# Strassen's blocks in every matrix multiply of a conv-and-MLP layer, and all engines in source order

## The chip, the core and the metric

One core of a Trainium2 chip runs the kernel. Five engines work side by side, each through its own list of instructions in order: TensorE (PE, matrix products into PSUM banks), VectorE (DVE), ScalarE (ACT), GpSimd (POOL, idle here) and SyncE (SP, which issues the transfers). The metric is the device time of one execution in microseconds (us).

## The reference

One layer on x of 512 tokens by 2048 channels, float32 throughout:

```
h = rms_norm(x, norm_mix)
b, c, v = split(h @ w_in, 3)             # w_in: 2048 x 6144
x = x + (b * conv3(c * v)) @ w_out       # causal, 3 taps per channel; w_out: 2048 x 2048
h = rms_norm(x, norm_mlp)
x = x + (relu(h @ w1) ** 2) @ w2         # w1: 2048 x 8192, w2: 8192 x 2048
```

## The kernel before, in words

Each number of an operand is split into a high part `hi` (the rounded value, a cast on ACT) and a rest `lo` (DVE subtracts); a product is three matmuls: hi by hi, hi by lo, lo by hi. All operands are kept with channels on the partitions and tokens along the row.

The four multiplies are cut into 96 blocks of 2048 weight rows by 256 weight columns: 24 of `w_in`, 8 of `w_out`, 32 of `w1`, 32 of `w2` (4 chunks `ch` of 8). A *plain* block (`plain`, `unit`) takes 96 matmuls of 512 columns. A *fast* block (`fast`, `quarters`) is one level of Strassen's algorithm in Winograd's form. The weights' quarters and their sums S1 to S4 (on DVE) give seven operands. They meet seven *forms* of the activations: the quarters Y11, Y21, Y22 and the differences T1 to T4. Each of the seven products has 24 matmuls of 256 columns, 168 a block; their results are added in PSUM or in tile `c` on ACT (copies) and DVE (adds). Before, the 24 blocks of `w_in` and the 8 of `w_out` are plain, the 64 of `w1` and `w2` fast.

`load` fetches the weights of a block (2 MB in four DMAs, tile `r`, two of them). `operand` makes `whi` and `wlo` for one seventh (or, in a plain block, one quarter) in a ring of three tiles (`RING`): the cast of one operand has to wait until the matmuls of the third operand before it are done. The normed input stays in SBUF (`h_hi`, `h_lo`), as does the gated conv (`g_hi`, `g_lo`). `w_out`'s results leave as forms: Y11, Y21, Y22 are split at once, T1 to T4 go through DRAM (`t_mid`). `w1`'s results go to DRAM (`hidden`, eight arrays a piece); at each chunk of `w2` the seven forms are read back (`read`: one DMA of 1 MB, a cast and a subtraction of 128x2048). `differences` makes the T forms in four DVE instructions. RMS factors (`token_factors`) are applied to results, since a factor per token can be pulled out of the product. Nothing in the code fixes the order: a scheduler places each engine's instructions by their dependencies and the order of the source.

Of the kernel before, what the change touches and what calls it, by code (L numbers as in the profile page):

```python
# [36 lines left out]
def trunk_kernel(  # L37
# [33 lines left out]

    dram = ctx.enter_context(tc.tile_pool(name="dram", bufs=1, space=bass.MemoryType.DRAM))
# [10 lines left out]
    cst.tile([P, 224], F32, name="lead")  # L83
    edge = ctx.enter_context(tc.tile_pool(name="edge", bufs=1, side="right"))
    edge.tile([P, 8], F32, name="edge")
# [4 lines left out]
    ssq = cst.tile([P, S], F32, name="ssq")  # L90

# [14 lines left out]
    def squares(xk, first, pool):  # L106
        if first:
            act.activation(ssq, xk, AF.Square)
        else:
            sq = pool.tile([P, S], F32, tag="sq", name="sq")  # L110
            act.activation(sq, xk, AF.Square)
            dve.tensor_tensor(out=ssq, in0=ssq, in1=sq, op=ALU.add)

    def token_factors(pool, tag):


        total = bank()
        pe.matmul(total, ones, ssq, start=True, stop=True)
        m, t = (pool.tile([P, S], F32, tag=tag, name=n) for n in ("m", "t"))
# [23 lines left out]
    def unit(acc, r, k0, a_hi, a_lo, k_first=False):  # L143

        hi, lo = operand(r[:, k0 : k0 + QK, :], [P, QK, GC])
        js, ks = range(2), range(QK)
        for j, k in [(j, k) for k in ks for j in js] if k_first else [(j, k) for j in js for k in ks]:
            cs = slice(j * P, (j + 1) * P)
            a, b = a_hi[:, k0 + k, :], a_lo[:, k0 + k, :]
            first, last = k0 + k == 0, k0 + k == KT - 1  # L150
            pe.matmul(acc[j], hi[:, k, cs], a, start=first, stop=False)  # L151
            pe.matmul(acc[j], hi[:, k, cs], b, start=False, stop=False)  # L152
            pe.matmul(acc[j], lo[:, k, cs], a, start=False, stop=last)  # L153

    def plain(w, c0, a_hi, a_lo):
        acc = [bank() for _ in range(2)]
        r = load(w, 0, c0)
        for k0 in range(0, KT, QK):
            unit(acc, r, k0, a_hi, a_lo)
        return acc  # L160

    def quarters(r, early):
# [11 lines left out]
        tt(s_a, x21, x22, ALU.add)  # L174
        yield X11, operand(x11, shape)
        if early:
            yield X12, operand(x12, shape)
        tt(s_b, s_a, x11)
        yield S1, operand(s_a, shape)
        yield S2, operand(s_b, shape)  # L180
        tt(s_a, x12, s_b)
        yield S4, operand(s_a, shape)
        tt(x21, x11, x21)
        yield S3, operand(x21, shape)
        if not early:
            yield X12, operand(x12, shape)
        yield X22, operand(x22, shape)

    def fast(r, forms, c, early=False):


        bx, by, bz = (bank()[:, :HS] for _ in range(3))
        sums = {X11: bx, S1: bz, S2: bx, S4: bz, S3: bx, X12: by, X22: bx}
        t0, t1 = slice(0, HS), slice(HS, S)
        for i, (hi, lo) in quarters(r, early):
            acc = sums[i]
            f_hi, f_lo = forms[i]
# [5 lines left out]
            if i == X11:  # L203
                act.copy(c[:, 0, t0], acc)
            elif i == S1:
                act.copy(c[:, 1, t1], acc)
            elif i == S2:
                act.copy(c[:, 0, t1], acc)
            elif i == X22:
                act.copy(c[:, 1, t0], acc)  # L210
            else:
                o = {S4: c[:, 0, t1], S3: c[:, 1, t1], X12: c[:, 0, t0]}[i]
                dve.tensor_tensor(out=o, in0=acc, in1=o, op=ALU.add)  # L213

    def differences(q):
# [12 lines left out]
    rows = cw.tile([5 * KT, P], F32, name="rows", bufs=1)


    dve.memset(ones, 1.0)
    dve.memset(rows, 0.0)
    make_identity(nc, ident)
    act.dma_start(rows[:KT], norm_mix[0].rearrange("(k p) -> k p", p=P))
    act.dma_start(rows[KT : 2 * KT], norm_mlp[0].rearrange("(k p) -> k p", p=P))
    act.dma_start(rows[2 * KT :], conv_w[0].rearrange("t (k p) -> (t k) p", p=P))

    warm = bank()
    for _ in range(WARM):
        pe.matmul(warm[:, :P], ones, ones, start=True, stop=True)  # L240
    pc = bank()
    pe.transpose(pc[:, : 5 * KT], rows, ident[: 5 * KT, : 5 * KT])
    dve.tensor_copy(par[:, : 5 * KT], pc[:, : 5 * KT])

    parts = [D, 2 * D, 0]
    acc_n = [[bank() for _ in range(2)] for _ in range(2)]
    r_n = [wp.tile([P, KT, GC], F32, tag="r", name="r") for _ in range(2)]
    XK = XC // P
    with tc.tile_pool(name="xin", bufs=2, side="right", reuse_waits="tile") as xin:
        for c in range(D // XC):  # L250
# [10 lines left out]
            for j in range(0, XK, 2):  # L261
                xs = xin.tile([P, 2, S], F32, tag="xs", name="xs")
                for i in range(2):
                    kt = c * XK + j + i
                    pt = bank()
                    for b in range(S // P):
# [3 lines left out]
                    act.activation(h_hi[:, kt, :], pt, AF.Copy, scale=gain(0, kt))  # L270
                    dve.scalar_tensor_tensor(  # L271
                        out=h_lo[:, kt, :], in0=pt, scalar=gain(0, kt),
                        in1=h_hi[:, kt, :].bitcast(F32), op0=ALU.mult, op1=ALU.subtract,
                    )
                    dve.tensor_copy(xs[:, i, :], pt)
                    squares(xs[:, i, :], kt == 0, cw)
                nc.sync.dma_start(x_res[(c * XK + j) // 2], xs.rearrange("p i t -> p (i t)"))
            for i in range(2):
                unit(acc_n[i], r_n[i], c * XK, h_hi, h_lo, k_first=c == 0)
        token_factors(cw, "sq")  # L280

    with tc.tile_pool(name="gp", bufs=1, side="right", reuse_waits="tile") as gp:
        g_hi = gp.tile([P, KT, S], F32R, name="g_hi")
        g_lo = gp.tile([P, KT, S], F32R, name="g_lo")
        gp.tile([P, 112], F32, name="behind")


        pad = 16
        for n in range(NG):
            def part(i):  # L290
                if n == 0 and i < 2:
                    return acc_n[i]
                return plain(w_in, parts[i] + n * GC, h_hi, h_lo)

            acc_c = part(0)
            us = []
            for j in range(2):
                u = cw.tile([P, pad + S], F32, tag="u", name="u")
                dve.memset(u[:, pad - 2 : pad], 0.0)
                dve.tensor_tensor(out=u[:, pad:], in0=acc_c[j], in1=rbc, op=ALU.mult)  # L300
                us.append(u)
            acc_v = part(1)
            cvs = []
            for j in range(2):
                kt, u = n * 2 + j, us[j]
                cv = cw.tile([P, S], F32, tag="cv", name="cv")
                dve.tensor_tensor(out=cv, in0=acc_v[j], in1=rbc, op=ALU.mult)
                dve.tensor_tensor(out=u[:, pad:], in0=u[:, pad:], in1=cv, op=ALU.mult)
                act.activation(cv, u[:, pad - 2 : pad - 2 + S], AF.Copy, scale=tap(0, kt))
                for i in (1, 2):  # L310
                    dve.scalar_tensor_tensor(
                        out=cv, in0=u[:, pad - 2 + i : pad - 2 + i + S], scalar=tap(i, kt), in1=cv,
                        op0=ALU.mult, op1=ALU.add,
                    )
                dve.tensor_tensor(out=cv, in0=cv, in1=rbc, op=ALU.mult)
                cvs.append(cv)
            acc_b = part(2)
# [130 lines left out]
```

## Time and profile before

| | us |
|---|---|
| median of 3 runs (2020.28 to 2022.25) | 2021.81 |
| the profiled execution | 2022.01 |
| its span, first to last instruction | 2020.2 |
| PE busy | 1971.8 (98%) |
| DVE busy | 1416.3 (70%) |
| ACT busy | 841.9 (42%) |

The mean granted TensorE clock is 0.988 of full speed. PE works on `w_in` until about 535 us (its first two blocks are done at 62 us, beside the transposes of x), on `w_out` until 713, on `w1` until about 1350 and on the four chunks of `w2` to the end. Matmuls are pipelined: one is shown as busy from its start to its modelled end and the next starts before that, so the pace is read from a count of matmuls over a stretch and not from the duration of one.

### The profile page before, as it was taken

The numbers are of one execution on the slowest core, as the hardware profiler recorded it, in microseconds if no ns is written. First come the engines' busy times: TensorE is split into PE (matmuls) and PEld (weight loads), VectorE is DVE, ScalarE is ACT, GpSimd is POOL, SyncE is SP. The second block draws the span as 40 slices with busy tenths as digits, with TensorE's granted clock in tenths as the row PEclk, the third lists the DMA queues.
The fourth block names the chain that finished last, engine by engine and source line by source line (L and its number), as shares of the span: only waits on it lengthen the run. The fifth ranks groups of instructions, "written<-read, shape, count | busy, mean of one in ns | idle before, by whom it ended". The sixth has DMA issues, their size and how long they took to land.

```text
span 2020.2 us, 32807 instructions
## 1 busy us (share of the span) xinstructions
PE 1971.8 (98%) x14001; PEld 1843.0 (91%) x14001; DVE 1416.3 (70%) x1541; ACT 841.9 (42%) x1036; POOL 0.7 (0%) x6
## 2 busy tenths in 40 slices
PE   9999999999999979999999999989998998998998
PEld 8888888888888879999999999979998998998998
DVE  6643244334444588888888888888788879789875
ACT  5322222222233344544545445445455446446444
POOL 0000000000000000000000000000000000000000
PEclk9999999999999989999999999989999999999999
DMA  8322322322444454444454444467558448446542
GB/s 281 136 84 84 125 85 84 122 87 84 140 153 167 175 179 173 161 168 157 160 185 147 167 179 156 168 224 255 168 171 270 164 168 285 159 161 210 177 138 82
DMA packets 260113, 325.12 MB, mean 161 GB/s; under 512 B 9008, under 2 KB 242560, under 8 KB 255872
## 3 DMA queue, kind: packets, MB, share of 16 engines
q1 hardware_dynamic: 255616, 318.80, 46.0%
q10 hardware_dynamic: 4352, 4.24, 0.7%
q8 instruction: 109, 1.79, 0.4%
q14 instruction: 36, 0.29, 0.0%
HBM read 260.09 MB, written 62.91 MB: 160 GB/s over the span
## 4 chain that ended last, share of the span: by engine, by line
PE 89%; DMA 4%; DVE 3%; ACT 2%; issue 1%; SPq 0%; ACTq 0%; DVEq 0%
PE acc L200 18%; PE acc L202 18%; PE acc L201 18%; PE acc L152 11%; PE acc L153 11%; PE acc L151 11%; DMA f<-hidden 1%; DVE flo L101 1%; DMA r<-in_mlp_w_dram 1%; DVE wlo L101 1%; ACT whi L100 1%; DMA r<-in_conv_w_in_dram 1%; ACT fhi L100 1%; DMA f<-t_mid 0%; DVE c L410 0%
## 5 line engine op out<-in xcount | busy, mean ns | idle before, releaser
L200 PE MATMUL acc<-fhi,whi 128*128 128x256 f32 x3584 | 1000.3, 279 | 18.5 <-ACT fhi L100 16.4
L202 PE MATMUL acc<-fhi,wlo 128*128 128x256 f32 x3584 | 999.5, 279 | 17.0 <-DVE wlo L101 16.8
L201 PE MATMUL acc<-flo,whi 128*128 128x256 f32 x3584 | 999.0, 279 | 5.5 <-DVE flo L101 5.5
L101 DVE TENSOR_TENSOR wlo<-r,whi 128x1024 fp32r<-128x1024 f32 x384 | 468.7, 1223 | 385.7 <-ACT whi L100 376.7
L100 ACT CAST whi<-r 128x1024 fp32r<-128x1024 f32 x384 | 405.1, 1055 | 723.6 <-PE acc L152 376.3
L200 PEld LDWEIGHTS acc<-fhi,whi 128*128 128x128 f32 x3584 | 680.6, 190 | 20.2 <-ACT fhi L100 17.0
L202 PEld LDWEIGHTS acc<-fhi,wlo 128*128 128x128 f32 x3584 | 680.3, 190 | 18.7 <-DVE wlo L101 18.6
L201 PEld LDWEIGHTS acc<-flo,whi 128*128 128x128 f32 x3584 | 680.5, 190 | 8.1 <-DVE flo L101 8.0
L100 ACT CAST whi<-s 128x1024 fp32r<-128x1024 f32 x192 | 202.3, 1054 | 308.7 <-PE acc L201 219.0
L152 PE MATMUL acc<-h_lo,whi 128*128 128x512 f32 x768 | 298.8, 390 | 0.3 <-DVE h_lo L271 0.2
L153 PE MATMUL acc<-h_hi,wlo 128*128 128x512 f32 x768 | 298.8, 389 | 0.0
L151 PE MATMUL acc<-h_hi,whi 128*128 128x512 f32 x768 | 298.1, 390 | 0.5 <-ACT h_hi L270 0.4
L101 DVE TENSOR_TENSOR wlo<-s,whi 128x1024 fp32r<-128x1024 f32 x192 | 234.9, 1223 | 50.9 <-ACT whi L100 50.9
L152 PEld LDWEIGHTS acc<-h_lo,whi 128*128 128x128 f32 x768 | 144.1, 188 | 31.7 <-DVE h_lo L271 1.5
L151 PEld LDWEIGHTS acc<-h_hi,whi 128*128 128x128 f32 x768 | 143.8, 188 | 31.1 <-ACT h_hi L270 0.8
L153 PEld LDWEIGHTS acc<-h_hi,wlo 128*128 128x128 f32 x768 | 144.1, 188 | 29.8
L213 DVE TENSOR_TENSOR c<-acc,c 128x256 f32<-128x256 f32 x192 | 81.1, 423 | 76.9 <-PE acc L202 76.2
L151 PE MATMUL acc<-g_hi,whi 128*128 128x512 f32 x256 | 99.6, 389 | 0.0
L152 PE MATMUL acc<-g_lo,whi 128*128 128x512 f32 x256 | 99.6, 389 | 0.0
L153 PE MATMUL acc<-g_hi,wlo 128*128 128x512 f32 x256 | 99.6, 389 | 0.0
L172 DVE TENSOR_TENSOR s<-r 128x1024 f32<-128x1024 f32 x64 | 78.1, 1220 | 7.1 <-DMA r<-in_mlp_w_dram 6.4
L172 DVE TENSOR_TENSOR s<-r,s 128x1024 f32<-128x1024 f32 x64 | 78.4, 1225 | 2.0
(66 smaller groups left out, 1002.2 us busy)
## 6 DMA issues: line engine op xcount, KB each, us to landing
r<-in_mlp_w_dram SPq DMA_DIRECT2D x256, 512.0 KB, 5.5
r<-in_conv_w_in_dram SPq DMA_DIRECT2D x96, 512.0 KB, 6.0
hidden<-q SPq DMA_DIRECT2D x32, 1024.0 KB, 3.9
f<-hidden SPq DMA_DIRECT2D x28, 1024.0 KB, 6.9
r<-in_conv_w_out_dram SPq DMA_DIRECT2D x32, 512.0 KB, 5.6
xt<-x_mid SPq DMA_DIRECT2D x32, 512.0 KB, 4.3
x_mid<-c SPq DMA_DIRECT2D x24, 512.0 KB, 2.9
xn<-in_x_dram SPq DMA_DIRECT2D x16, 256.0 KB, 5.0
```

Source lines behind the costliest of these rows:

```text
L100: act.copy(hi, src)
L101: dve.tensor_tensor(out=lo, in0=src, in1=hi.bitcast(F32), op=ALU.subtract)
L151: pe.matmul(acc[j], hi[:, k, cs], a, start=first, stop=False)
L152: pe.matmul(acc[j], hi[:, k, cs], b, start=False, stop=False)
L153: pe.matmul(acc[j], lo[:, k, cs], a, start=False, stop=last)
L172: dve.tensor_tensor(out=o, in0=a, in1=b, op=op)
L200: pe.matmul(acc, hi[:, k, :], f_hi[:, k, :], start=first, stop=False, skip_group_check=True)
L201: pe.matmul(acc, hi[:, k, :], f_lo[:, k, :], start=False, stop=False, skip_group_check=True)
L202: pe.matmul(acc, lo[:, k, :], f_hi[:, k, :], start=False, stop=last, skip_group_check=True)
L213: dve.tensor_tensor(out=o, in0=acc, in1=o, op=ALU.add)
```

## The change

88 of the 96 blocks are now fast. Plain are the two blocks of `w_in` in the prologue, two more at the start of `w_in` and its last, the first and the last of `w_out` and the first of `w1`.

The forms live in fixed places: `quart` holds the four quarters, `sums` T2 and T3, `last_sum` T4; T1 shares the place of Y12. A plain block reads all four quarters, a fast one Y11, Y21, Y22 and T1 to T4. For the fast blocks of `w_in`, `x` is read back from `x_res`, scaled and subtracted into T1 to T4 (`fetch_h`, `normed_quarter`, `settle_h`). The gated conv goes out to DRAM (`gated`) and the input of the MLP too (`normed`), with their differences; `pass_over` reads each back while the plain blocks on either side of the border run. `exchange` does it for `w2`.

The work is a list of `steps`, a seventh of a fast block or a quarter of a plain one. All engines' instructions are given in source order (`tc.manual_schedule()`): in iteration i come the matmuls of step i, the outputs of step i-1, the weights' sum of step i+3, the operand of step i+2, and whatever `at(i, ...)` put there (loads, reads, splits, what follows a block).

```diff
+LEAD = 2
+HOME = {Y11: 0, Y12: 1, T1: 1, Y21: 2, Y22: 3}
-    t_mid = dram.tile([NP, P, 4, HS], F32, name="t_mid")
+    gated = dram.tile([NP, P, 8, HS], F32, name="gated")
+    normed = dram.tile([NP, P, 8, HS], F32, name="normed")
+    quart = [cst.tile([P, 4, NP, HS], F32R, name=f"q_{n}") for n in ("hi", "lo")]
+    sums = [cst.tile([P, 2, NP, HS], F32R, name=f"t_{n}") for n in ("hi", "lo")]
+    last_sum = [cst.tile([P, NP, HS], F32R, name=f"u_{n}") for n in ("hi", "lo")]
...
     def differences(q):
-        for o, a, b in ((4, 1, 0), (5, 3, 4), (6, 3, 1), (7, 2, 5)):
-            dve.tensor_tensor(out=q[:, o, :], in0=q[:, a, :], in1=q[:, b, :], op=ALU.subtract)
+        tt(slice(4, 8, 2), slice(1, 4, 2), slice(0, 2))
+        tt(5, 3, 4)
+        tt(7, 2, 5)
...
+        at(loads[-2]["end"] - LEAD - 1 if len(loads) > 1 else -1, lambda: box.update(r=load(w, r0, c0)))
...
+        for i in (X11, X12, S2, S1, S3, S4, X22) if late else range(7):
+            steps.append((
+                lambda i=i: add(i),
+                lambda i=i: box["made"][1][i](),
+                lambda op, i=i: multiply(op, i),
+                lambda i=i: out(i),
+            ))
...
+    def pass_over(last, first, src):
+        s, f, box = last["start"], first["start"], {}
+        at(s - 2, fetch_pairs, box, src, 0, 2)
+        at(s, fetch_pairs, box, src, 2, 2)
+        at(s + 1, settle_pairs, box, 0, 2)
+        at(s + 1, fetch_pairs, box, src, 4, 2)
+        at(s + 2, settle_pairs, box, 2, 2)
+        at(s + 3, settle_pairs, box, 4, 2)
+        at(s + 3, fetch_pairs, box, src, 6, 1)
+        at(f, settle_pairs, box, 6, 1)
+        at(f, settle_last, last)
+        box = {}
+        at(f + 1, fetch, box, src, T2)
+        at(f + 2, fetch, box, src, T3)
+        at(f + 3, settle, box, T2)
+        at(f + 3, fetch, box, src, T1)
+        at(f + 3, settle, box, T3)
+        at(f + 3, fetch, box, src, T4)
+        at(f + 4, settle, box, T1)
+        at(f + 6, settle, box, T4)
+    def exchange(start, src, reads):
+        for i in range(7):
+            at(start + reads[i], fetch, box, src, i)
+        for i, t in enumerate((2, 3, 4, 6, 9, 10, 11)):
+            at(start + t, settle, box, i)
+    def conv(n, box_c, box_v, d):
...
+        at(e, product)
+        at(e + d, factor)
+        at(e + d + 1, taps)
+    def gate(n, box_v, box, d):
...
+            tt(box["c"], box["c"], box_v["cv"], ALU.mult)
+            tt(q[:, :4, :].rearrange("p (i h) t -> p i (h t)", h=2), box["c"], wide(rbc), ALU.mult)
+        at(box["end"] + d, product)
+        at(box["end"] + d, lambda: differences(box["q"]))
+        at(box["end"] + d + 1, keep, box, gated[n])
...
+    with tc.manual_schedule():
+        extra(-1)
+        made = []
+        for i in range(-LEAD - 1, len(steps)):
+            if i >= 0:
+                steps[i][2](made.pop(0))
+            if i >= 1:
+                steps[i - 1][3]()
+            if i + LEAD + 1 < len(steps):
+                steps[i + LEAD + 1][0]()
+            if 0 <= i + LEAD < len(steps):
+                made.append(steps[i + LEAD][1]())
+            if i >= 0:
+                extra(i)
```

What stands on the engines in a row changes at three places. The first is DVE at the border between two chunks of `w2`, before: `flo<-f` is the split of a form, `wlo` the split of an operand, L172 a sum of weights, L213 an add of a result, L410 the residual.

```order
L172 TENSOR_TENSOR r<-r 128x8x128
L101 TENSOR_TENSOR flo<-f,fhi 128x2048
L101 TENSOR_TENSOR wlo<-r,whi 128x1024
L101 TENSOR_TENSOR flo<-f,fhi 128x2048
L213 TENSOR_TENSOR c<-acc,c 128x256
L101 TENSOR_TENSOR wlo<-r,whi 128x1024 x2
L213 TENSOR_TENSOR c<-acc,c 128x256
L101 TENSOR_TENSOR flo<-f,fhi 128x2048
L213 TENSOR_TENSOR c<-acc,c 128x256
L101 TENSOR_TENSOR flo<-f,fhi 128x2048 x2
L410 TENSOR_TENSOR c<-c,xt 128x1024
```

The same place in the changed kernel, where L179 is the sum, L279 the add, L357 the residual and `q_lo`, `t_lo` the forms:

```order
L357 TENSOR_TENSOR c<-c,xt 128x1024
L121 TENSOR_TENSOR q_lo<-f,q_hi 128x2048
L121 TENSOR_TENSOR wlo<-r,whi 128x1024
L121 TENSOR_TENSOR q_lo<-f,q_hi 128x2048
L279 TENSOR_TENSOR c<-acc,c 128x256
L121 TENSOR_TENSOR wlo<-r,whi 128x1024
L121 TENSOR_TENSOR t_lo<-f,t_hi 128x2048
L279 TENSOR_TENSOR c<-acc,c 128x256
L179 TENSOR_TENSOR s<-r 128x1024
L121 TENSOR_TENSOR wlo<-r,whi 128x1024
L279 TENSOR_TENSOR c<-acc,c 128x256
L179 TENSOR_TENSOR s<-s,r 128x1024
```

Before, the seven forms stand within 15 rows, two of them side by side; now within 25, with the split of an operand between any two.

The second is DVE in the stage of `w_in`, before, in plain blocks (L300 scales a result by the factor of its token, `u` and `cv` are the conv):

```order
L101 TENSOR_TENSOR wlo<-r,whi 128x1024 x3
L300 TENSOR_TENSOR u<-acc,rbc 128x512 x2
L101 TENSOR_TENSOR wlo<-r,whi 128x1024 x4
L307 TENSOR_TENSOR cv<-acc,rbc 128x512
L308 TENSOR_TENSOR u<-u,cv 128x512
```

And now, around the end of a trio of fast blocks (L357 the gate's two products, L193 the differences):

```order
L121 TENSOR_TENSOR wlo<-r,whi 128x1024
L357 TENSOR_TENSOR c<-c,cv 128x1024
L357 TENSOR_TENSOR q<-c,rbc 128x1024
L193 TENSOR_TENSOR q<-q 128x2x256
L193 TENSOR_TENSOR q<-q 128x256 x2
L121 TENSOR_TENSOR wlo<-r,whi 128x1024
L279 TENSOR_TENSOR c<-acc,c 128x256
L121 TENSOR_TENSOR wlo<-r,whi 128x1024
L279 TENSOR_TENSOR c<-acc,c 128x256
L179 TENSOR_TENSOR s<-r 128x1024
```

The sums of weights and the adds of results have come into this stage; there were none.

The third is SP at the border from `w_out` to `w1`, before (`xt` the residual's tiles):

```order
L134 DMA r<-in_mlp_w_dram 128x4x256 x4
L349 DMA x_mid_67<-xt 128x1024
L354 DMA t_mid<-q 128x1024
L365 DMA f<-t_mid 128x8x256 x4
L134 DMA r<-in_mlp_w_dram 128x4x256 x4
L407 DMA xt<-x_mid_67 128x1024 x2
```

And in the changed kernel at the border from `w_in` to `w_out`, which now works in the same way:

```order
L311 DMA f<-gated 128x1024
L360 DMA gated<-q 128x2048
L302 DMA f<-gated 128x8x256
L403 DMA xt<-x_res 128x2x512
L146 DMA r<-in_conv_w_out_dram 128x4x256 x4
L302 DMA f<-gated 128x8x256 x3
```

The four reads of differences stood in one piece behind the last write; now the first stands ahead of the next weights and three behind them.

## Rows read from the trace of the kernel before

**Rows 1.** Page, part 1: busy time (share of span) and instructions.

```profile
PE 1971.8 (98%) x14001; PEld 1843.0 (91%) x14001; DVE 1416.3 (70%) x1541; ACT 841.9 (42%) x1036; POOL 0.7 (0%) x6
```

**Rows 2.** Busy time of each engine in stretches; instructions in brackets, then clock, DMA.

```profile
core 0: us, PE busy (x) PEld busy (x) DVE busy (x) ACT busy (x) POOL busy (x), PEclk, DMA share, GB/s
75.00:320.00 245.00, 245.00 (x1083) 202.86 (x1082) 97.72 (x119) 57.68 (x61) 0.00 (x0) 1.00 0.30 101
...
713.00:750.00 37.00, 26.46 (x173) 23.65 (x172) 32.22 (x33) 19.67 (x22) 0.00 (x0) 0.82 0.53 176
750.00:1330.00 580.00, 580.00 (x5076) 580.00 (x5075) 502.36 (x576) 283.32 (x362) 0.00 (x0) 1.00 0.47 167
1330.00:1400.00 70.00, 56.33 (x444) 55.04 (x444) 58.40 (x56) 37.66 (x39) 0.00 (x0) 0.90 0.77 257
...
1500.00:1560.00 60.00, 54.28 (x451) 53.28 (x450) 56.62 (x48) 35.58 (x38) 0.00 (x0) 0.97 0.76 257
...
1660.00:1720.00 60.00, 54.06 (x442) 53.41 (x442) 56.31 (x47) 35.25 (x38) 0.00 (x0) 0.94 0.81 271
...
1820.00:1880.00 60.00, 54.78 (x452) 54.33 (x451) 55.89 (x49) 35.38 (x37) 0.00 (x0) 0.94 0.65 220
```

**Rows 3.** Who PE waited for: total us, times, longest.

```profile
PE acc L202 <- DVE wlo L101: 16.8, 5, 5.4
PE acc L200 <- ACT fhi L100: 16.4, 3, 8.3
PE acc L201 <- DVE flo L101: 5.5, 4, 2.3
```

**Rows 4.** PE in order of time, first transposes, third block's start: start us, duration.

```profile
8.81 1.91 PE L267 MATMUL acc<-ident,xn 128*128 128x128 f32 x16
...
62.25 0.80 PE L151 MATMUL acc<-h_hi,whi 128*128 128x512 f32 x1
```

**Rows 5.** Chain that ended last, in order of time: a finish, the tail.

```profile
1892.14 0.87 PE acc L394 x8
...
2012.73 0.38 ACT c L210
```

**Rows 6.** DVE in order of time, 1000 to 1020 us: start, duration, idle before.

```profile
1003.00 1.22 DVE L379 SCALAR_TENSOR_TENSOR c<-c,rbc 128x1024 f32<-128x1024 f32 x1
1004.14 1.22 DVE L172 TENSOR_TENSOR s<-r 128x1024 f32<-128x1024 f32 x1
...
1006.41 1.09 DVE L219 TENSOR_TENSOR q<-q 128x256 f32<-128x256 f32 x3
1007.41 1.22 DVE L172 TENSOR_TENSOR s<-s,r 128x1024 f32<-128x1024 f32 x1
```

**Rows 7.** DVE in order of time, 1365 to 1380 us.

```profile
1376.44 2.29 DVE L101 TENSOR_TENSOR flo<-f,fhi 128x2048 fp32r<-128x2048 f32 x1
1378.64 0.42 DVE L213 TENSOR_TENSOR c<-acc,c 128x256 f32<-128x256 f32 x1
```

**Rows 8.** ACT in order of time, 1505 to 1512 us.

```profile
1507.46 1.94 ACT L100 CAST fhi<-f 128x2048 fp32r<-128x2048 f32 x1
1509.27 0.40 ACT L208 COPY c<-acc 128x256 f32<-128x256 f32 x1
1509.53 1.09 ACT L100 CAST whi<-r 128x1024 fp32r<-128x1024 f32 x1
```

**Rows 9.** Chain at the border to w1: write and read of t_mid.

```profile
719.48 2.67 DMA t_mid<-q
...
722.71 7.89 DMA f<-t_mid
```

**Rows 10.** Stretches of 10 us at a border of w2, columns as in rows 2.

```profile
1520.00:1530.00 10.00, 5.00 (x27) 4.58 (x27) 9.88 (x8) 5.94 (x6) 0.00 (x0) 0.83 1.07 376
1680.00:1690.00 10.00, 4.62 (x32) 4.41 (x32) 9.21 (x8) 5.92 (x6) 0.00 (x0) 0.80 1.09 369
```

More of the change, by code (lines that the diff above doesn't have):

```diff
@@ L187, in quarters @@
[L187 to L193, printed above, removed]
-        t0, t1 = slice(0, HS), slice(HS, S)
-        for i, (hi, lo) in quarters(r, early):
-            acc = sums[i]
-            f_hi, f_lo = forms[i]
+        add = {
+            S1: lambda: tt(s_a, x21, x22, ALU.add),
+            S2: lambda: tt(s_b, s_a, x11),
+            S4: lambda: tt(s_a, x12, s_b),
+            S3: lambda: tt(x21, x11, x21),
+        }
@@ new lines, in fast, with add, multiply @@
+    def fast(w, r0, c0, late=False):
+        box = new_block(w, r0, c0, 7)
+        t0, t1 = slice(0, HS), slice(HS, S)
+        def add(i):
+            if "made" not in box:
+                box["made"] = quarters(box["r"])
+            if late and i in (S1, S2):
+                if i == S2:
+                    box["made"][0][S1]()
+                    box["made"][0][S2]()
+            else:
+                box["made"][0].get(i, lambda: None)()
+        def multiply(op, i):
+            if i == X11:
+                bx, by, bz = (bank()[:, :HS] for _ in range(3))
+                box["acc"] = {X11: bx, S1: bz, S2: bx, S4: bz, S3: bx, X12: by, X22: bx}
+            acc = box["acc"][i]
+            hi, lo = op
+            f_hi, f_lo = form(i)
@@ L228, in trunk_kernel @@
[L228 to L241, printed above, removed]
@@ L359, in trunk_kernel @@
-    fb = ctx.enter_context(tc.tile_pool(name="fb", bufs=1, side="right", reuse_waits="tile"))
-    home = {i: fa if i in (Y11, Y21, Y22) else fb for i in range(7)}
-    def read(i, src, pool):
-        f = pool.tile([P, NP, HS], F32, tag="q", name="f", bufs=3)
-        nc.sync.dma_start(f, src.rearrange("k p t -> p k t"))
-        made = form(home[i], i)
-        split(*made, f)
-        return made
-    mw = ctx.enter_context(tc.tile_pool(name="mw", bufs=2, reuse_waits="tile"))
-    for i, k in ((T1, 0), (T2, 1), (T3, 2), (T4, 3)):
-        forms[i] = read(i, t_mid[:, :, k, :], mw)
@@ new lines, in normed_quarter @@
+    def normed_quarter(box, i):
+        for k in range(NP):
+            act.activation(box[i][:, k, :], box[i][:, k, :], AF.Copy, scale=gain(0, 2 * k + (i in (Y21, Y22))))
+    boxes = [{"end": 0}, {"end": 0}]
+    at(0, early)
+    trios = []
+    for n in range(NG):
+        trio = []
+        for i in range(3):
+            if n == 0 and i < 2:
+                trio.append(boxes[i])
+            elif (n, i) in ((0, 2), (1, 0), (NG - 1, 2)):
+                trio.append(plain(w_in, 0, parts[i] + n * GC))
+            else:
+                trio.append(fast(w_in, 0, parts[i] + n * GC, late=(n, i) == (1, 1)))
+            if i == 1:
+                conv(n, *trio, 0 if n in (0, NG - 1) else 2)
+        gate(n, *trio[1:], 0 if n in (0, NG - 1) else 2)
@@ new lines, in trunk_kernel @@
+    for n in range(NG):
+        if n in (0, NG - 1):
+            box = plain(w_out, 0, n * GC)
+        else:
+            box = fast(w_out, 0, n * GC, late=n == 1)
+        if n == 0:
+            pass_over(in_last, box, gated)
+        if n == NG - 1:
+            back = {}
+            at(box["start"] - 8, fetch, back, gated, Y12)
+            at(box["start"] - 4, settle, back, Y12)
+        residual(n, box, 0 if n >= NG - 2 else 2)
+    for n in range(DFF // GC):
+        last, box = box, fast(w1, 0, n * GC, late=n == 1) if n else plain(w1, 0, n * GC)
+        if n == 0:
+            pass_over(last, box, normed)
+            at(box["start"] + 2, token_factors, lambda name: tile_x(name)[:, 0, :S])
+        if n == DFF // GC - 1:
+            exchange(box["start"], hidden[0], (-2, -1, 2, 3, 4, 5, 6))
+        squared_relu(n, box)
```

430 lines of the change are left out of this document (251 added, 179 removed).

## The prediction

> **What bounds the kernel now.** First the page: PE is busy for 98% of the span, DVE for 70%, ACT for 42% [rows 1]. So TensorE is the bound, and two questions follow: how many matmuls at which pace, and where PE stands still.
>
> The pace comes from the stretches [rows 2]. From 75 to 320 us there are only plain blocks and PE never pauses: 245 us / 1083 = 0.2262 us a matmul, 96 x 0.2262 = 21.72 us a plain block. From 750 to 1330 us there are only fast blocks: 580 us / 5076 = 0.1143 us, 168 x 0.1143 = 19.20 us a fast block, 19.20 / 7 = 2.74 us a step. That pace already holds whatever small waits a block has.
>
> The standstills come from the same view. In the five stretches at the borders the time is longer than matmuls x 0.1143: 37 - 173 x 0.1143 = 17.2 us (`w_out` to `w1`), 70 - 444 x 0.1143 = 19.3 (`w1` to `w2`), and 8.5, 9.5 and 8.3 between the chunks of `w2`: 62.8 us in all. The waits of PE name the culprits [rows 3]: operands and forms that ACT and DVE had not made, 38.7 us; the rest is the lower clock after a pause (0.80 to 0.83 in such a stretch [rows 10]).
>
> The account closes. The third block's first matmul starts at 62.25 us [rows 4]. After it come 30 plain blocks (651.6), 64 fast (1228.8), the transposes of eight finished column blocks (8 x 0.87 = 7.0 [rows 5]), the 62.8 of standstill, and the tail of 2020.2 - 2012.7 = 7.5 us [rows 5]: 2020.0 of 2020.2 us.
>
> **The change part by part.**
>
> *24 blocks made fast.* 24 x (21.72 - 19.20) = -60.4 us. Nothing covers this term: PE is the bound in those stretches [rows 2]. It supposes that the form's place and the stage don't matter to a matmul; the shapes are those of the fast blocks now.
>
> The weight loads beside the matmuls are busy for all of the 580 us in the fast stretch, against 202.86 of 245 in the plain one [rows 2]: a matmul of 256 columns has as many weights to load as one of 512. The Trainium skill (TensorE: Matmul & The Clock Gate, section on the back-to-back issue gap) gives N/2.4 + 2.5 ns a matmul, so 215.8 and 109.2 ns, where the rows have 226 and 114; by the page a swap would bring 24 x (20.72 - 18.35) = 56.9 us in place of 60.4. The measured paces decide.
>
> *The same work moved onto DVE.* A fast block costs DVE 11 full-width instructions (7 splits, 4 sums) and 3 adds. DVE starts such instructions 1.14 us apart although each is shown with 1.22; three of a quarter's width take 1.00, so 0.33 each, and a split of a form 2.20 [rows 6, 7]. A fast block is 11 x 1.14 + 3 x 0.33 = 13.5 us of DVE; a trio of `w_in` adds the product, the factor, four taps of half width (at most 1.14 each), the gate's two products and the differences (1.3): 40.6 + 2.3 + 4.6 + 2.3 + 1.3 = 51.1 us at most, against 57.6 us of PE. In `w1` a block has 13.5 + 1.14 + 1.3 = 16 of 19.2, and there PE doesn't wait [rows 2]. So I cost this at nothing. The worst step is the gate's: 1.14 + 2.28 + 1.3 = 4.7 us against 2.74; the 2.0 too much are gone two steps later, where DVE has 1.14 a step. An operand is made two steps ahead, so it may be late by 2 x 2.74 less its own chain of at most 2.7: 2.8 us. If this cover fails, the loss is that of the rival below. Even with the full 1.22 in place of 1.14 a trio stays under 57.6.
>
> *Start of the fast blocks in `w_in`.* Reading x back and making T1 to T4 stands on ACT and DVE beside eight plain steps of 21.72 / 4 = 5.43 us. What falls into the first fast steps is two form splits and one difference of that width, 6.6 us, beside 1.14 to 2.6 a step: the lag reaches about 4.4 us at the third fast step, with 2.8 to 4 free. I take 1 us (0 to 6.6). The head up to 62.25 us keeps its instructions and their order.
>
> *`exchange`, three times in `w2`.* From the step of the first form's split to the end of the next block are 12 steps, 32.9 us of PE. DVE has there the splits of 12 operands, 8 sums, 2 residuals, 7 forms and 6 adds: step by step 4.5, 3.3, 3.7, 2.6, 4.8, 2.3, 2.3, 4.5, 3.3, 3.7, 2.6, 2.6 = 40.2 us. That is 7.3 too much. Of it 2.3 us is hidden by the lead: the product X22 may not write its bank before DVE has added S3 from it, one step (2.74) less the add's 0.42. So 5 us are lost, plus about 1 for forms that are themselves late (T3, Y21 and T4 are split only two steps before their use): 6 us each, 18 in all, against 26.3 now. Bounds: 0 (the spreading hides all) and 9.5 each, as now. The transfers hardly decide: two blocks' weights (2.1 MB each), seven forms (1.05 each) and four residual tiles (0.5 each) are 13.6 MB in the 15 steps or 41 us from the first read on, 330 GB/s, where the transfers reached 376 [rows 10]; that is near enough that a late read could add 1 or 2 us.
>
> *`w1` to `w2`.* The same, but the last two blocks of `w1` also bring two times 1.3 us of differences into the 12 steps: 6 + 2.6 = 8.6, against 19.3 now, of which some 8 was a single wait for a form's cast (16.4 us in three such waits [rows 3]); `exchange` reads the first form four steps ahead of its split. Bounds 5 and 19.3.
>
> *`pass_over`, `w_in` to `w_out`.* New. The quarters come back during plain steps, where DVE has 1.14 + 2.2 of 5.43 us. The differences are the critical part: the last gate ends about 7 us into the first plain block, its write and the read of T2 take 10.9 us as at `t_mid` [rows 9], so T2 is there at 18, and T3 behind it and behind 2 MB of weights (3 MB at up to 376 GB/s [rows 10]) at 24 to 26. ACT stands at T3's cast (1.81 [rows 8]) with the operand of the second next step queued behind it, so that operand is ready at about 29 and is due at 4 x 5.43 + 2 x 2.74 = 27.2. With T4's split and the first residual in the step after (7 us of DVE), I take 4 us. Bounds: 0, and 17.2 as at the `t_mid` border, which has the same write and read without plain steps to cover them.
>
> *`pass_over`, `w_out` to `w1`.* The same with the RMS factors' chain in it, some 6.5 us of DVE two steps before T2's split, and two sums of weights: 7 us, for 17.2 now. Bounds 0 and 17.2.
>
> *Transfers and SP.* All stand in source order. A block's weights are asked for as soon as their tile is free, eight steps (22 us) before their first use, for 2.1 MB, which is 16 us even at the 7.9 us that a read of 1 MB took [rows 9]; a wait ahead of them in SP's row would have to pass 6 us to matter.
>
> **The sum.** 62.25 + 6 x 21.72 (130.3) + 88 x 19.20 (1689.6) + 7.0 + 7.5 = 1896.7 us, and standstills of 1 + 4 + 7 + 8.6 + 18 = 38.6: a span of 1935.3 us. The profiled execution lies 1.8 us over its span (2022.01 against 2020.2), and 0.2 over the median: 1937 us.
>
> **The rivals.**
>
> *The borders stay as dear as now* (and the new one costs 17.2): 1896.7 + 62.8 + 17.2 + 1.8 = 1978 us. For it: DVE has the same forms to split, and DVE was the last to arrive in most waits [rows 3]. Against: plain blocks now lie at two borders, and the forms are spread.
>
> *The borders are hidden nearly whole*: standstills of 8 us, 1907 us. For it: ACT and DVE are free for a good part of the block before. Against: 40.2 us of DVE in 32.9 us of PE.
>
> *The clock falls at the new borders.* A pause of some 5 us was followed by 0.80 to 0.83 of full clock over 10 us, i.e. 3.4 to 4 us at the lower of the two levels (1.2 GHz) and 1.7 to 2 us lost [rows 10]. If each of the 20 or so short pauses of the new kernel did this, it would be 40 us: 1977 us. Against: those 1 to 2 us pauses are not the 5 us ones of the rows. The Trainium skill (TensorE: Matmul & The Clock Gate, section on a second failure mode) describes such frequent short pauses between groups of matmuls as enough to make the clock swing; no row here shows it.
>
> *Source order lets DVE set the pace in every fast block: slower.* In iteration i the sum and the operand stand behind an output that waits for PE, so DVE cannot work ahead of the ring. As soon as DVE's work and waits in a block pass 19.2 us, each of the 88 blocks is paced by DVE; the gain of 85 us is gone when a block takes 19.20 + 85 / 88 = 20.2 us, or 0.14 us a step. With a block at 20.5 us: 2049 us. Against: 16 us in the heaviest block, and `w1` runs without a wait today at that load [rows 2].
>
> **How the numbers follow.** Forecast 60%; borders as now 14%, hidden 12%, clock 5%, slower 5%, and 4% for a failure of the swap itself (fast blocks in `w_in` no quicker than plain ones), about 2000 us. A measurement tells 0.2% (4 us) from no change. All but the slower rival and a share of the last are faster: 0.93 faster, 0.02 same, 0.05 slower. Range: from 1905, the hidden borders, to 1982, which takes in the dear ones and the clock.
>
> **What would show it.** Right: 88 blocks at 19.2 us in every stretch without a border, `w_in`'s too; PE's waits only at the six borders, by name for the splits of operands and forms, 30 to 50 us in all; the clock at 1.00 between. Wrong: a stretch of `w_in` with fast blocks over 19.5 us and PE waiting for DVE; a first wait of 5 us or more at a border on a read or a write of DRAM; a clock under 0.95 in a stretch of `w_in`.

## The result, and the profile after

The changed kernel takes 2008.94 us (median of 3 runs, 2008.15 to 2011.45) against 2021.81: a ratio of 0.9941 with an interval of 0.9918 to 0.9964, 0.6% faster. The forecast was 1937 us, its range 1905 to 1982: the sign was right, the time is 72 us above it and outside the range. The profiled execution took 2011.45 us, its span is 2009.6.

First the page's busy times, which answer to [rows 1]:

```profile
PE 1938.7 (96%) x15729; PEld 1890.8 (94%) x15729; DVE 1650.4 (82%) x1686; ACT 977.5 (49%) x1232; POOL 0.7 (0%) x6
```

PE is busy for 33 us less than before, and of the span it is idle for 71 us in place of 48. Whom it waited for (total us, times, longest) answers to [rows 3]:

```profile
PE acc L267 <- ACT c L281: 27.7, 9, 8.1
PE acc L267 <- DVE c L279: 22.1, 9, 5.9
PE acc L269 <- DVE wlo L121: 4.8, 3, 2.5
PE acc L165 <- ACT whi L120: 2.6, 2, 1.9
...
PE acc L167 <- DVE wlo L121: 1.5, 3, 0.8
PE acc L268 <- DVE q_lo L121: 1.3, 4, 0.3
PE acc L268 <- DVE t_lo L121: 1.3, 3, 0.5
```

Here is the surprise. Before, PE waited 38.7 us for operands and forms (`wlo`, `fhi`, `flo`). Those are now worth 11.5 us. Fifty microseconds go to `c`: PE waits for *results* to be taken out of PSUM, copies on ACT (L281) and adds on DVE (L279), so that it may write the bank again. Before, that kind of wait was next to nothing:

```profile
PE acc L200 <- ACT c L208: 1.2, 3, 0.5
```

The stretches (columns as in [rows 2]) show where:

```profile
118.00:150.00 32.00, 23.01 (x173) 22.37 (x173) 22.33 (x19) 17.04 (x24) 0.00 (x0) 0.84 0.26 88
150.00:480.00 330.00, 330.00 (x2890) 330.00 (x2890) 293.71 (x314) 152.39 (x201) 0.00 (x0) 1.00 0.39 133
...
750.00:1320.00 570.00, 570.00 (x4921) 570.00 (x4921) 477.76 (x527) 274.38 (x350) 0.00 (x0) 1.00 0.47 163
1320.00:1400.00 80.00, 67.09 (x520) 66.07 (x520) 66.66 (x62) 40.95 (x44) 0.00 (x0) 0.91 0.70 241
1500.00:1560.00 60.00, 55.40 (x465) 54.67 (x464) 56.53 (x49) 35.65 (x38) 0.00 (x0) 0.97 0.72 253
```

From 150 to 480 us `w_in` runs at 330 / 2890 = 0.1142 us a matmul, the pace the forecast used. The start of that stage loses 32 - 173 x 0.1143 = 12.2 us, the border to `w2` 20.6, one border inside `w2` 6.9; two more of these follow at the same size. The stretch of `w1` runs at 0.1158, 7.5 us more than at 0.1143. Not all of a loss is standstill: in the stretch from 118 us PE is idle for 9.0 of the 12.2, at the border to `w2` for 12.9 of the 20.6. The rest is the same matmuls at a lower clock.

PE in order of time gives the first matmul of each stage, 512 columns in a plain block, 256 in a fast one:

```profile
116.46 0.28 PE L267 MATMUL acc<-q_hi,whi 128*128 128x256 f32 x1
...
498.58 0.40 PE L165 MATMUL acc<-q_hi,whi 128*128 128x512 f32 x1
...
543.39 0.28 PE L267 MATMUL acc<-q_hi,whi 128*128 128x256 f32 x1
...
675.73 0.40 PE L165 MATMUL acc<-q_hi,whi 128*128 128x512 f32 x1
...
721.40 0.28 PE L267 MATMUL acc<-q_hi,whi 128*128 128x256 f32 x1
```

From these starts, and those of the first experiment below, comes the account by stage, beside the forecast's terms (us):

| stage | forecast | after | e1 |
|---|---|---|---|
| head, two plain blocks of `w_in` | 62.25 + 43.4 = 105.7 | 116.5 | 109.5 |
| 19 fast blocks of `w_in` | 364.8 + 1 = 365.8 | 382.1 | 374.2 |
| two plain blocks | 43.4 | 44.8 | 44.8 |
| 6 fast blocks of `w_out`, first border | 115.2 + 4 = 119.2 | 132.3 | 122.3 |
| two plain blocks | 43.4 | 45.7 | 45.7 |
| 63 fast blocks, other borders, transposes, tail | 1209.6 + 33.6 + 14.5 = 1257.7 | 1288.2 | 1250.5 |
| span | 1935.3 | 2009.6 | 1947.0 |

A *parked* instruction is one that waits at the head of its engine's row, so that what stands behind it waits too. What it does is seen on ACT at the start of the fast blocks, in order of time (start, duration, idle before and its releaser):

```profile
110.12 1.91 ACT L120 CAST t_hi<-f 128x2048 fp32r<-128x2048 f32 x1 [6.93 <-DVE f L357]
111.94 2.00 ACT L120 CAST whi<-r 128x1024 fp32r<-128x1024 f32 x2
122.86 3.30 ACT L547 ACTIVATE f<-f,par 128x256 f32<-128x256 f32 x8 [8.92 <-DMA f<-x_res]
126.07 1.04 ACT L232 COPY c<-acc 128x512 f32<-128x512 f32 x2
127.01 1.04 ACT L120 CAST whi<-s 128x1024 fp32r<-128x1024 f32 x1
127.95 1.90 ACT L120 CAST q_hi<-f 128x2048 fp32r<-128x2048 f32 x1
129.75 0.36 ACT L281 COPY c<-acc 128x256 f32<-128x256 f32 x1
```

L547 scales a quarter of x read back from DRAM; ACT stands 8.92 us for that read. Behind it, in row, is the copy of the first product, X11, whose matmuls ended about 119.2 us. The next product but one writes the same bank and would have started at 121.9; it starts at 130.17. That is the longest wait of the kernel, and no operand is late in it.

### The profile page after: what moved, and what is told of

Same layout as the page of the kernel before. It is cut to its first block, busy times and chain, and to the rows that moved or that the text cites. A ratio compares the mean times of both kernels' runs of the same rounds, so it can differ in the third digit from the quotient of the medians.

```text
span 2009.6 us, 36810 instructions
## 1 busy us (share of the span) xinstructions
PE 1938.7 (96%) x15729; PEld 1890.8 (94%) x15729; DVE 1650.4 (82%) x1686; ACT 977.5 (49%) x1232; POOL 0.7 (0%) x6
## 5 line engine op out<-in xcount | busy, mean ns | idle before, releaser
L267 PE MATMUL acc<-q_hi,whi 128*128 128x256 f32 x2816 | 781.6, 278 | 3.0 <-ACT c L281 3.0
L269 PE MATMUL acc<-q_hi,wlo 128*128 128x256 f32 x2816 | 780.5, 277 | 2.8 <-DVE wlo L121 2.8
L268 PE MATMUL acc<-q_lo,whi 128*128 128x256 f32 x2816 | 780.8, 277 | 1.3 <-DVE q_lo L121 1.3
L267 PEld LDWEIGHTS acc<-q_hi,whi 128*128 128x128 f32 x2816 | 531.5, 189 | 3.3 <-ACT c L281 3.2
L269 PEld LDWEIGHTS acc<-q_hi,wlo 128*128 128x128 f32 x2816 | 529.7, 188 | 3.3 <-DVE wlo L121 3.2
L268 PEld LDWEIGHTS acc<-q_lo,whi 128*128 128x128 f32 x2816 | 530.3, 188 | 2.3 <-DVE q_lo L121 2.1
L267 PE MATMUL acc<-t_hi,whi 128*128 128x256 f32 x1408 | 398.5, 283 | 24.7 <-ACT c L281 24.7
L269 PE MATMUL acc<-t_hi,wlo 128*128 128x256 f32 x1408 | 395.7, 281 | 2.0 <-DVE wlo L121 2.0
L268 PE MATMUL acc<-t_lo,whi 128*128 128x256 f32 x1408 | 395.8, 281 | 1.3 <-DVE t_lo L121 1.3
L281 ACT COPY c<-acc 128x256 f32<-128x256 f32 x352 | 130.2, 370 | 422.7 <-PE acc L269 407.4
L267 PEld LDWEIGHTS acc<-t_hi,whi 128*128 128x128 f32 x1408 | 270.8, 192 | 27.2 <-ACT c L281 27.2
L267 PE MATMUL acc<-u_hi,whi 128*128 128x256 f32 x704 | 203.6, 289 | 22.2 <-DVE c L279 22.1
```

What stands on the lines that cost most here:

```text
L267: pe.matmul(acc, hi[:, k, :], f_hi[:, k, :], start=first, stop=False, skip_group_check=True)
L268: pe.matmul(acc, hi[:, k, :], f_lo[:, k, :], start=False, stop=False, skip_group_check=True)
L269: pe.matmul(acc, lo[:, k, :], f_hi[:, k, :], start=False, stop=last, skip_group_check=True)
L281: act.copy(o, acc)
```

## The experiments

Two theories stood against each other. P (place in the row): the work fits, but in source order a result stands behind something that is parked or long, and has one step of 2.74 us where an operand has two. (Three of a block's four reuses of a bank wait for a copy on ACT: S2 after X11, S4 after S1, S3 after S2. The fourth, X22 after S3, waits for an add on DVE.) W (work): DVE has too much to do at the borders, whatever the order. All runs are compared with the kernel before on the same chip, 2021.1 to 2022.4 us.

**e1: the scheduler's order on the changed code.**

```diff
-    with tc.manual_schedule():
+    if True:
```

> The changed kernel's blocks, pools and text, but a scheduler places each engine's instructions, as before the change, in place of source order. Theory P (parked rows): the 74 us over the forecast come from ACT and DVE standing at an instruction that waits, for a read from DRAM or for each other, while the copies and adds of results, which PE needs within one step, stand behind it in source order. A scheduler that moves results ahead would bring the borders down to what they cost before: 1897 us of blocks, head and tail plus 63 to 80 of standstill, 1960 to 1980 us. Theory W (work): DVE simply has more to do at the borders than PE's time there allows, in whatever order: within 1% of the changed kernel, 1990 to 2025 us.

1948.16 us (1947.53 to 1954.68), ratio 0.9645 (0.9629 to 0.9662): the same instructions, 61 us less than in source order, and 12 us below the range that P gave. Its page and waits:

```profile
PE 1912.9 (98%) x15729; PEld 1866.8 (96%) x15729; DVE 1645.3 (85%) x1686; ACT 978.4 (50%) x1232; POOL 0.7 (0%) x6
```

```profile
PE acc L268 <- DVE q_lo L121: 6.2, 6, 2.3
PE acc L267 <- DVE c L279: 4.7, 7, 0.9
...
PE acc L267 <- ACT c L281: 2.3, 1, 2.3
```

DVE does 1645 us of work, as in source order (1650), in a span 63 us shorter, and the waits for `c` fall from 49.8 to 7.0 us. P holds, and W falls as a bound for the whole. Of the 63 us of span, 37 are idle time of PE (71 against 34), and 26 are busy time: PE is busy 1938.7 us in source order and 1912.9 here, for the same matmuls. The account now closes within 12 us of the forecast, so little of the swap's 60 us can be missing. The scheduler also moves the transfers; how much of the 61 us is their part this run doesn't separate.

DVE in order of time at a border inside `w2`, first in source order:

```profile
1502.33 1.22 DVE L357 TENSOR_TENSOR c<-c,xt 128x1024 f32<-128x1024 f32 x1
1503.46 2.29 DVE L121 TENSOR_TENSOR q_lo<-f,q_hi 128x2048 fp32r<-128x2048 f32 x1
1505.66 1.22 DVE L121 TENSOR_TENSOR wlo<-r,whi 128x1024 fp32r<-128x1024 f32 x1
1506.80 2.29 DVE L121 TENSOR_TENSOR q_lo<-f,q_hi 128x2048 fp32r<-128x2048 f32 x1
1509.00 0.42 DVE L279 TENSOR_TENSOR c<-acc,c 128x256 f32<-128x256 f32 x1
1509.34 1.22 DVE L121 TENSOR_TENSOR wlo<-r,whi 128x1024 fp32r<-128x1024 f32 x1
1510.47 2.28 DVE L121 TENSOR_TENSOR t_lo<-f,t_hi 128x2048 fp32r<-128x2048 f32 x1
1512.67 0.41 DVE L279 TENSOR_TENSOR c<-acc,c 128x256 f32<-128x256 f32 x1
```

and from the same second form on in e1:

```profile
1453.05 2.29 DVE L121 TENSOR_TENSOR q_lo<-f,q_hi 128x2048 fp32r<-128x2048 f32 x1
1455.25 1.23 DVE L121 TENSOR_TENSOR wlo<-r,whi 128x1024 fp32r<-128x1024 f32 x1
1456.39 0.42 DVE L279 TENSOR_TENSOR c<-acc,c 128x256 f32<-128x256 f32 x1
...
1468.60 1.23 DVE L357 TENSOR_TENSOR c<-c,xt 128x1024 f32<-128x1024 f32 x1
```

In source order the residual (L357) stands ahead of the forms, the adds are pushed back, and the last product of the block, released by the add that starts at 1512.67, starts 2.6 us late. The scheduler has put the residual behind the fourth form, since nothing waits for it.

**e2: source order alone**, `w_in` and `w_out` plain as before.

```diff
-            elif (n, i) in ((0, 2), (1, 0), (NG - 1, 2)):
+            elif True:
...
-            pass_over(in_last, box, gated)
+            pass_over(in_last, box, gated, sums_too=False)
```

> Source order with the leads of the changed kernel, but all blocks of w_in and w_out plain as before the change (x is not read back for differences, and the gated conv comes back as quarters alone). Blocks, head and tail are then 1957 us by the forecast's paces. Theory P: the start of w_in and the border to w_out lose their waits (some 45 us of the changed kernel's standstills), the borders to w1 and of w2 keep theirs, about 60 to 70 us: 2017 to 2030 us, no better than before the change. Theory F (the new fast blocks themselves are dear, source order is not): the borders cost less than before, about 40 us: 1995 to 2005 us.

2043.73 us, ratio 1.0112 (1.0097 to 1.0127): slower than before by 22 us, and above the ranges of both theories. Its borders lose 14.5 us into `w1`, 18.4 into `w2` and about 7 inside `w2`, a little less than before. Most of the 22 us is another thing: a plain matmul takes 160 / 688 = 0.2326 us in its plain stretch, against 0.2262 [rows 2], some 19 us over 30 plain blocks. So its time says little of the order itself; the comparison of e1 with the changed kernel does. Its waits say more: without any fast block in `w_in` or `w_out`, PE waits for results where it waited for operands before.

```profile
PE acc L267 <- DVE c L279: 19.7, 8, 5.8
PE acc L267 <- ACT c L281: 9.0, 4, 4.6
```

**e3: reads earlier, the first gate later**, source order kept: the reads of x one to five steps earlier, two T forms' reads right behind T2's at both borders of `pass_over`, the first gate four steps later (not in the cut below).

```diff
-    at(1, fetch_h, Y22)
+    at(0, fetch_h, Y22)
...
-    at(5, fetch_h, Y21)
+    at(3, fetch_h, Y21)
...
-    at(in_last["start"] - 9, fetch_h, Y12)
+    at(in_last["start"] - 14, fetch_h, Y12)
```

> The changed kernel with reads moved ahead in SP's row and nothing else: the third quarter of x at once with the first two, the fourth as soon as the first tile is free (for which the first gate comes four steps later), Y12 of x five steps earlier, T3 and T1 of the gated and normed arrays right behind T2 and ahead of the next weights. Theory P: the pauses of 8.3, 3.1 and 3.9 us behind these reads, and part of the 5 us at 95 to 104 us, go: 1988 to 1995 us. Theory W: the same work stands in the same rows, so 2005 to 2012 us.

1986.7 us, ratio 0.9827 (0.9811 to 0.9843): 22 us less than the changed kernel. The pause of 8.3 us at the start is 3.0, the one at 485 us is gone. PE's waits for ACT's copies fall from 27.7 to 18.2 us; those for DVE's adds stay, at 22.0. ACT, at the same place:

```profile
109.73 1.28 ACT L232 COPY c<-acc 128x512 f32<-128x512 f32 x2 [0.82 <-PE acc L167]
...
118.58 0.37 ACT L281 COPY c<-acc 128x256 f32<-128x256 f32 x1 [4.81 <-DVE q L357]
```

The copy of X11 no longer waits behind a read; now ACT stands 4.81 us for a product of the gate on DVE, which this run has moved back. Reads on which a row is parked, with the gate's place, are about a third of what the order costs.

**e4: the forms' low part left out** at the four borders into and inside `w2`.

```diff
-            at(start + t, settle, box, i)
+            at(start + t, lambda i=i: act.copy(form(i)[0], box.pop(i)))
```

> Leaves out DVE's split of the seven forms (the low part) at the four borders of w2; ACT's cast and the reads stay, so 7 x 2.2 us of DVE are gone from each. Theory W for these borders: their 44 us of standstill (21.5 and three times 7.5) fall under 10, 1970 to 1978 us. Theory P: the waits of ACT for reads and for DVE's residuals stay, at least 25 of the 44: 1990 to 1998 us.

1974.7 us, ratio 0.977 (0.9756 to 0.9785): 34 us less, in the range of W. PE's waits for DVE's adds fall from 22.1 to 2.2 us; those for ACT's copies stay, at 26.6. The border inside `w2`, in one stretch:

```profile
1480.00:1540.00 60.00, 60.00 (x527) 60.00 (x527) 48.05 (x48) 38.71 (x42) 0.00 (x0) 1.00 0.84 294
```

No idle, 0.1139 us a matmul. So at these borders the 2.3-us splits are what the results stand behind. For these borders W is right that DVE's work is what is late. But e1 shows that the same splits in another order cost only about half (60 - 493 x 0.1143 = 3.7 us in e1's stretch, 6.9 in source order). Together with e3, this splits the 49.8 us: the adds' 22.1 lie almost all at the borders of `w2`, the copies' 27.7 in part behind reads.

**e5: e1 and e3 together.** 

> The scheduler in place of source order (1948 us by itself) and the reads moved ahead (22 us less in source order). If the reads cost the same 20 us under a scheduler, 1926 to 1932 us; theory P says that a scheduler had already moved the results past the parked reads, so that only the 2.4 us pause at the start of w_in is left to gain: 1941 to 1948 us.

1949.01 us (1948.14 to 1950.08), ratio 0.9637 (0.9625 to 0.965): no gain over e1. The scheduler had already put other work ahead of the parked rows, as P says.

**e7: each product in a PSUM bank of its own**, source order; the sum over the products is left out.

```diff
-                bx, by, bz = (bank()[:, :HS] for _ in range(3))
-                box["acc"] = {X11: bx, S1: bz, S2: bx, S4: bz, S3: bx, X12: by, X22: bx}
+            box.setdefault("acc", {})[i] = acc = bank()[:, :HS]
```

> The changed kernel in source order, where each of the seven products of a fast block starts in a PSUM bank of its own (the sum over products in a bank is left out, so results are not the reference's; instructions, reads and the order stay). A copy or an add of a result then has seven steps of time and no longer one. Theory P, with the results' one step as what PE runs into: PE's waits for c (27.7 us for copies, 22.1 for adds) go, and part of them, say 15 to 25 us, comes back as waits for operands behind the same parked instructions: 1970 to 1990 us. If the lead of two steps for operands is as tight as the results', the waits only change their name: 2000 to 2010 us.

1993.57 us, ratio 0.9859 (0.9845 to 0.9874): 15 us less, a little above the range that P gave. The waits for `c` are gone, but:

```profile
PE acc L266 <- DVE wlo L121: 29.7, 21, 2.6
PE acc L264 <- ACT whi L120: 12.6, 5, 5.6
PE acc L265 <- DVE t_lo L121: 3.9, 4, 1.3
```

When the bank no longer stops PE, the next operand does, at the same places: the rows are late as a whole, and the result's one step is only the first deadline that they miss. `w1` returns to its pace, 570 / 4989 = 0.1143 us a matmul from 750 to 1320 us; so the 7.5 us there belong to shared banks in source order. The time from one block of `w1` to the next (by the starts of its product on DVE) says the same: 19.47 us in the changed kernel, 19.20 here, and 19.20 in e1, which shares the banks but not the order.

**e8: the forms' low parts on GpSimd** at the `w2` borders, on top of e5.

```diff
-            at(start + t, settle, box, i)
+            at(start + t, settle_pool, box, i)
```

> As the scheduler with early reads, and GpSimd, idle until now, makes the low part of the seven forms at the four borders of w2. If DVE's work is what is left at these borders and GpSimd takes up to 6 us for one: 10 to 15 us less than that kernel, 1928 to 1935 us. If GpSimd is slower than that, or slows DVE beside it, the forms come late: 1950 us or more.

2036.15 us, ratio 1.0069 (1.0051 to 1.0088): 87 us slower than e5. GpSimd, then DVE, in order of time:

```profile
1487.41 5.64 POOL L311 TENSOR_TENSOR q_lo<-f,q_hi 128x2048 fp32r<-128x2048 f32 x1
```

```profile
1488.47 0.41 DVE L279 TENSOR_TENSOR c<-acc,c 128x256 f32<-128x256 f32 x1
1488.81 5.33 DVE L121 TENSOR_TENSOR wlo<-r,whi 128x1024 fp32r<-128x1024 f32 x1
```

A split of an operand, 1.22 us elsewhere, takes 5.33 and ends about 1 us after GpSimd's instruction has ended (1487.41 + 5.64 = 1493.05, and 1488.81 + 5.33 = 1494.14): DVE stood still through it. The add, which reads PSUM, keeps its 0.41. The work was not moved off DVE, it was made longer on it.

**e6, e9, e10, e11, e12: the plain matmul's 0.233 us.** e6 is e2 with all matmuls of one column half ahead of those of the other, so that PE no longer changes the PSUM bank every three matmuls; e9 and e10 are e1 and e2 with a row's four quarters side by side; e11 and e12 besides write the operand as one row of 512 columns.

```diff
-            plain_products(box["acc"], op, k0, k_first=True)
+            plain_products(box["acc"], op, k0, k_first=False)
...
-    quart = [cst.tile([P, 4, NP, HS], F32R, name=f"q_{n}") for n in ("hi", "lo")]
+    quart = [cst.tile([P, NP, 4, HS], F32R, name=f"q_{n}").rearrange("p k q t -> p q k t") for n in ("hi", "lo")]
...
-            a, b = (quart[i][:, kt % 2 * 2 : kt % 2 * 2 + 2, kt // 2, :] for i in range(2))
+            a, b = (flat_quart[i][:, kt // 2, kt % 2 * S : kt % 2 * S + S] for i in range(2))
```

> Source order with plain blocks in w_in and w_out, as in the run of order alone (2044 us, where a plain matmul took 0.233 us in place of 0.227), but with the plain blocks' matmuls in the order of before: all of one column half, then the other, no longer changing the PSUM bank every three matmuls. If changing the bank is what slows them, the pace goes back to 0.2266 us and the time to 2024 us; if it is the operand's place (two rows of 256 columns), the time stays at 2044 us.

> The scheduler's order on the changed code (median 1948.2 us before this edit), and now the four quarters of an operand pair lie side by side in SBUF, so that a plain matmul reads one row of 512 columns instead of two rows of 256 that lie 8 KB apart. Theory L (the place of the operand makes a plain matmul 0.233 us instead of 0.2266): 6 plain blocks of 96 matmuls gain 0.0066 us each, 3.8 us: 1944 to 1945 us. Rival N (something else in the changed code slows the plain blocks): 1948 us, within 2. Against both: a fast matmul's row of 256 columns now lies 4 KB from the next one's instead of 1 KB, and the splits of a form write rows of 256 numbers apart; if that costs, 1955 us or more.

> Source order with w_in and w_out all plain (median 2043.7 us before this edit), with the quarters side by side as well. Theory L: some 30 plain blocks x 96 x 0.0066 = 19 us less, 2024 to 2026 us, and 0.2266 us a matmul in 160 to 320 us. Rival N: pace 0.233 and 2043 to 2046 us.

> Source order, w_in and w_out all plain, quarters side by side (median 2043.4 us before this edit; each plain matmul starts 0.2333 us after the one before, also with the place changed), and now the plain matmul's operand is written as one row of 512 columns instead of two rows of 256 that happen to touch. Theory R (what costs is the second row in the operand's description): 0.2266 us a matmul, some 30 plain blocks x 96 x 0.0067 = 19 us less, 2023 to 2026 us. Rival N (something else): 0.233 and 2042 to 2045 us.

> The scheduler's order on the changed code (1948 to 1950 us), quarters side by side and the plain operand written as one row. Theory R: 6 plain blocks x 96 x 0.0067 = 3.9 us less, 1944 to 1946 us. Rival N: 1948 to 1950 us.

2045.45, 1950.01 (1947.26 to 1950.55), 2043.36, 2044.35 and 1949.32 us (1946.16 to 1951.57). The pace in a plain stretch of e11:

```profile
160.00:320.00 160.00, 160.00 (x688) 128.90 (x687) 53.14 (x53) 39.34 (x46) 0.00 (x0) 1.00 0.34 115
```

688 matmuls, as in e2. Three guesses, three misses: neither the change of bank, nor the operand's place in a row, nor its description is the cause. The cause stays open. In the changed kernel it touches 6 blocks, 6 x 96 x 0.0067 = 3.9 us.

e1, e5, e9 and e12 agree within 2 us: the changed code in the scheduler's order beats the kernel before by 3.6% and the changed one by 3.0%.

## Why the prediction was wrong

**The swap was right.** It was to bring 60.4 us, at 0.1143 us a fast matmul in every stage; `w_in` has 0.1142, and e1's span comes within 12 us of the forecast. Rivals "swap fails" and "DVE sets the pace in every fast block" are out.

**The step that failed is the slack that was given to the rows in source order.** The prediction let every row of DVE and ACT be as late as an operand, "2 x 2.74 less its own chain of at most 2.7: 2.8 us", and cost the added rows at nothing on that ground. It named the shorter deadline, X22's bank after S3's add, once, in `exchange`, and took the lead from it there. But S2 after X11, S3 after S2 and S4 after S1 have the same deadline of one step, in all 88 blocks. Of the 61.3 us of waits in the rows above, 49.8 are for results. The deadline that it named is 22.1 of them, by the adds; the three that it did not name are 27.7, by the copies.

**Parked rows were priced as reads, not as what stands behind them.** For the start of `w_in` the prediction summed DVE's work and took 1 us (0 to 6.6). It asked what is "queued behind" a parked cast only for `pass_over`. ACT's L547 waits 8.92 us for x, with the copy of X11 behind it: the stage is 16.3 us over the forecast, and 10.8 more were lost ahead of it. Of these 1.8 are gone before the third block, though its head was to stay as it is (the matmul of the factors starts at 63.59 us, before at 61.79), and part where casts of plain operands stand behind the same line (at 90.64 us L547 waits 4.31 us for x, the cast behind it starts at 93.85, and PE 2 us late). e3 gives 22 us back by the places of the reads and of one gate.

**The borders.** Into `w_out` 4 us were forecast and the stage is 13.1 over that. PE stops twice, for 3.7 and 3.5 us, each time for a copy behind something parked on ACT, first a read and then the residual on DVE:

```profile
546.76 1.91 ACT L120 CAST t_hi<-f 128x2048 fp32r<-128x2048 f32 x1 [6.10 <-DMA f<-gated]
...
563.00 1.33 ACT L410 ACTIVATE q<-xt,par 128x512 f32<-128x512 f32 x2 [4.21 <-DVE xt L357]
```

`w_out` to `w1`: 7 forecast, about 14.5 measured (38.6 us from 721.4 us on, for 211 matmuls). `w1` to `w2`: 8.6 forecast, 20.6 measured, more than the 19.3 before. The three in `w2`: 18 forecast, about 21 measured. That is the one border where the prediction counted the rows step by step and had the right deadline: it forecast 6 us of waits each, and PE is idle for 4.6, most of it at X22. That the whole came so near is luck in part, since the other 2.3 us are the lower clock, which wasn't in the sum.

**The rest of the sum.** `w1`'s pace 7.5 us, the plain pace 3.9: neither was in it. Nor was the clock: the prediction put the part of the old 62.8 us that was not waits down to "the lower clock after a pause", but its own terms for the borders count rows of DVE and ACT alone. Of the 26 us by which PE is busy longer than in e1, some 8 are `w1`'s pace; the other 18, by this estimate, are the lower clock behind its pauses.

**The rival that came nearest** is "borders as dear as now" (1978 us), still 31 us short: it kept the old standstills but not the new place, the start of `w_in`. Two marks set for the wrong case did fire: PE waited 8.1 us behind a read of DRAM, though at the start of `w_in` and not at a border, and the clock was under 0.95 in a stretch of `w_in` (0.84). What misled was a cover tested on the wrong kernel: `w1` ran without a wait before, under the scheduler's order, and that was taken as evidence for the same load in source order.

**The clock** is 0.984 of full speed in the mean (0.988 before, 0.995 in e1). With the pause of 8.3 us in it, the stretch from 118 to 150 us has 0.84; with a pause of 2.6 us, 1500 to 1560 us has 0.97. The rival of a clock that falls at short pauses came in part. At e1's borders inside `w2`, with pauses of 0.2 to 0.9 us, the clock is 1.00 over the 60 us around them. But at e1's border into `w2` PE pauses five times in some 8 us, for 0.2 to 1.4 us each, and from 1320 to 1330 us the clock is 0.76, while PE doesn't stop at all. The stretch around it:

```profile
1300.00:1340.00 40.00, 35.73 (x277) 34.53 (x276) 37.04 (x34) 20.98 (x25) 0.00 (x0) 0.91 0.92 312
```

That border still loses 40 - 277 x 0.1143 = 8.3 us, and PE is idle for only 4.3 of them. The Trainium skill (TensorE: Matmul & The Clock Gate, section on a second failure mode) has frequent short pauses bring the clock to swing; the trace of e1 agrees at its border into `w2` and doesn't show it inside `w2`.

## What to carry to other kernels

When an order is written out by hand, give every row its own deadline: an operand's is the lead, a result's is the step after which its PSUM bank is written again, and the shortest of those behind a row is what that row may be late. A row that waits for DRAM holds everything behind it on its engine, so ask for the read early enough that it is never the last to come. And before an order by hand replaces a scheduler, run the same code under both: here that one edit was worth 61 us, as much as was forecast for the change of algorithm.

## What the runs showed of the hardware

- GpSimd's split of 128x2048 takes 5.37 us in the mean of 16, DVE's 2.29. In e8 a DVE instruction with two operands in SBUF stands still until the GpSimd one has ended (5.33 us for 1.22), and one that reads PSUM doesn't (0.41). The Trainium skill (SBUF — State Buffer, section "SBUF: two separate sides") says that the two share a pair of ports under an exclusive lock for the whole instruction; the trace agrees, and by that rule e8 needn't have been hopeful.
- Start to start, the plain matmul of 512 columns takes 0.2333 us in the changed code (e10, from 200 us on) and 0.2262 before, at a clock of 1.00 in both; bank order, layout and description of the operand were each tried and changed nothing.
- Pauses of 1.4 us and less were followed by a lower clock in one place of e1 (0.76 over 1320 to 1330 us, after five of them) and not in others (1.00 inside `w2`).
